# Dilated mixer: the values of two head groups projected as [dims, tokens] and turned by transposes, in place of products with strided stationary tokens

## The chip, the cores and the metric

The kernel runs on one core of one Trainium2 chip. The metric is the device time of one execution in microseconds, the median of several runs. Before the change it is 3231.49 us.

## The reference, cut to what matters

The network is an encoder of four layers for 512 tokens of width 1024 in float32. Each layer has a mixer and a SwiGLU block, each with a norm before and after it. The mixers are of kind A, B, C, A. The change touches kind A alone, which runs twice:

```python
def mixer_a(x, wqkv, wo):
    B, S, _ = x.shape
    qkv = (x @ wqkv).reshape(B, S, 3, A_NG, A_HEADS, A_HEAD_DIM)
    ...
    for g, (window, dilation) in enumerate(A_GROUPS):
        o, l = dilated_window_attention(qkv[:, :, 0, g], qkv[:, :, 1, g], qkv[:, :, 2, g], window, dilation, slopes[g])
    ...
    wgt = jax.nn.softmax(jnp.stack(lses, axis=0), axis=0)
    o = jnp.sum(wgt[..., None] * jnp.stack(outs, axis=0).astype(jnp.float32), axis=0)
    return o.reshape(B, S, -1).astype(x.dtype) @ wo
```

There are three groups (window and dilation 128 and 1, 512 and 4, 2048 and 16), each with 16 heads of 64 dims and with queries, keys and values of its own. In the second and third group a token sees only tokens at a distance that is a multiple of 4 or 16, so that one token in four forms a block of 128 that attends to itself.

## The kernel before, in words

Every product is made from float32 operands that are split into a high and a low part (`split`, L135: ScalarE copies the high part, VectorE subtracts it). `mm3` (L169) makes one product with three matmuls: high by high (L171), high by low (L172), low by high (L173). The normed input lies transposed in `yh` and `yl` as [dims, tokens], 8 slices of 128 dims (`KD`), 512 tokens and 64 more that repeat the first ones.

`wload` (L157) brings 1024 values a partition of weights from DRAM into a tile `raw` (3 buffers) by a DMA of SyncE, and splits it in two halves to `whi` and `wlo` (4 buffers each, L137 and L138).

Mixer A works by pairs of heads, p = 0 to 7. For each pair there are six projections of queries and keys (`proj_qk`, three groups, queries and keys): the weights stand still, 128 columns at a time, and the 512 tokens move. Each is 8 steps of three matmuls with 512 moving columns, into one PSUM bank of the tag "a" (the pool has 2 buffers for each tag). The values must come out with tokens as rows, so `vproj` lets the tokens stand still and moves the weights: 4 blocks of 128 tokens, 8 slices, three matmuls with 256 moving columns, 96 in all. `proj_v0` does this for the first group, once for four heads, with 128 tokens in order. `proj_v12` does it for groups two and three of one pair, and there a block is one token in four: `slice(c, S, 4)`. Its weights come as two tiles, each by two DMAs of 256 KB.

The order on TensorE is the emitted order. Attention goes in 64 units (pair, head, half of the blocks): `scores(n)`, `values(n - 2)`, `transposes(n - 1)`. Between these, `fill.run(part)` emits projection work from the generator `filler()` for as much estimated time as `part` says; a projection step of 0.65 us of estimate is yielded for each three matmuls with 512 columns or each six with 256. The order in `filler` is: queries and keys of group one (p+1), values of group one (every second pair), queries and keys of groups two and three (p+1), values of groups two and three (p+1). Buffers with one copy set gates: `wait(n)` stops the generator until unit n has been emitted. The second half of `proj_v12(p)` waits for unit 8p + 2, since `v12` of the pair before is read up to then; `proj_qk(p, 0, s)` waits for unit 8p - 5 before its bank is emptied. `fill.until` emits what a unit needs, without regard to the estimate. On ScalarE, VectorE and the queues a planner sets the order at build time.

`transposes` (L624) turns the softmax numerators by four transposes of 128 x 128 into one bank, and two splits move them to `pT`. `qk_evac` (L519) empties the banks of queries and keys; for groups two and three it reads the bank with a stride of four, `"p (l r) -> p r l"` (L534, L539).

Of the kernel before, what the change touches and what calls it, by code (L numbers as in the profile page):

```python
# [10 lines left out]
F32 = mybir.dt.float32  # L11
F32R = mybir.dt.float32r
AF = mybir.ActivationFunctionType
# [3 lines left out]
P = 128  # L17
S = 512
D = 1024
NB = S // P  # L20
KD = D // P
# [16 lines left out]
def const_tables():  # L38
    """Tables that depend on shapes alone."""
    f = np.float32  # L40
    q = np.arange(P)[:, None]
    w = np.arange(2 * P)[None, :]
    d0 = np.abs(w - 64 - q)
    t0 = np.where(d0 <= 64, d0, BIG).astype(f)
    l = np.arange(P)[None, :]
    d1 = np.abs(l - q)
    t1 = np.where(d1 <= 64, 4.0 * d1, BIG).astype(f)
    t2 = np.where((l - q) % 4 == 0, 4.0 * d1, BIG).astype(f)
    dist = np.concatenate([t0, t1, t2], axis=1)

    def angles(pos, dim):
        half = dim // 2
        fr = np.power(f(10000.0), -np.arange(half, dtype=f) * f(2.0) / f(dim)).astype(f)
        return (pos.astype(f)[:, None] * fr[None, :]).astype(f)

    t = np.arange(S)
    cs, sn = [], []
    for pos in (t // 64, t % 64):
        a = angles(pos, 64)
        c, s = np.cos(a), np.sin(a)  # L60
        cs += [c, c]
        sn += [-s, s]
    bcos = np.concatenate(cs, axis=1).astype(f)
    bsin = np.concatenate(sn, axis=1).astype(f)

    a = angles(t, 32)
    c, s = np.cos(a).astype(f), np.sin(a).astype(f)
    ccos = np.concatenate([c, c], axis=1)
    csin = np.concatenate([-s, s], axis=1)
    sc = f(96.0 ** -0.5)  # L70
    cq = np.empty((P, S), f)
    cq[:64] = -sc
    cq[64:96] = -(ccos.T * sc)
    cq[96:] = -(csin.T * sc)
    return {
        "t_dist": dist,
        "t_bcos": bcos,
        "t_bsin": bsin,
        "t_ckr": np.concatenate([ccos, csin], axis=1),
        "t_cq": cq,  # L80
    }


class Filler:
    """Work of the tensor engine that is emitted between the steps of something else."""
# [22 lines left out]
class Net:  # L108
# [32 lines left out]
    def behind(self, *ins):  # L141
        """What is emitted inside is issued after ins on their engines."""
        es = ExitStack()
        for i in ins:
            es.enter_context(self.tc.issue_after(i.ins))
        return es
# [10 lines left out]
    def wload(self, src, shape, pool=None, bufs=2):  # L157
        """Weights from DRAM as [128, ...] with at most 1024 values a partition, split."""
        n = int(np.prod(shape))
        raw, hi, lo = self.wtiles(pool, bufs)  # L160
        names = "abc"[: len(shape)]
        view = lambda x: x[:, :n].rearrange(
            f"p ({' '.join(names)}) -> p {' '.join(names)}", **dict(zip(names, shape)))
        self.nc.sync.dma_start(out=view(raw), in_=src)
        for c in (slice(0, n // 2), slice(n // 2, n)):
            self.split(hi[:, c], lo[:, c], raw[:, c])
        return view(hi), view(lo)
# [13 lines left out]
    def rstd(self, ss, n, count):  # L181
        """(ss / count + eps) ^ -0.5 for a [128, n] tile of sums."""
        nc = self.nc
        v = self.small.tile([P, 8], F32, tag="var", name=self.uid("var"))
        nc.vector.tensor_scalar(v[:, :n], ss, 1.0 / count, EPS, op0=ALU.mult, op1=ALU.add)
        r = self.small.tile([P, 8], F32, tag="rstd", name=self.uid("rstd"))
        nc.gpsimd.tensor_tensor(r[:, :n], v[:, :n], self.mhalf[:, :n], op=ALU.pow)
        return r
# [31 lines left out]
    def norm_t(self, t, yn, wrap):  # L220
        """Transposes of one block of tokens into yh, yl."""
# [13 lines left out]
    def rest(self, n=1):  # L235
        """Emits the loads of the next n blocks of the input."""
        for _ in range(min(n, len(self.loads))):
            self.loads.pop(0)()

    def flush(self, n=NB):  # L240
        """Emits the next n of the transposes that the stage before has left."""
        for _ in range(min(n, len(self.pending))):
            self.pending.pop(0)()

# [1 line left out]
    def rows_out(self, yp, stat, nf, w, acc_in, final, late=None, R=5):  # L246
        """y = stat^T @ w for [nf * 128, 1024] w. stat(f) gives the two parts [128, 512].
        final is None: the sums go to acc_in. Else (post gain, next pre gain or None, wrap).
        late: called before the products of the last f of the first half. A generator of PE time in us."""
        nc = self.nc  # L250
# [51 lines left out]
        # first half  # L302
# [26 lines left out]
        # second half  # L329
# [93 lines left out]
    def mixer_a(self, j, final):  # L423
        """Pairs of heads. The first group's blocks of queries are 128 tokens in order ("nat"), the other
        two groups share blocks of one token in four ("perm"). Both parts come out as [dims, tokens]."""
# [20 lines left out]
        def vproj(wt, dst, tok):  # L446
            for cp in range(2):
                bk = self.bank("a")
                for ci in range(2):
                    tb = tok(2 * cp + ci)  # L450
# [8 lines left out]
        def proj_v0(u):  # L459
            """Values of heads 4u..4u+3, first group: rows are keys."""  # L460
# [10 lines left out]
            g = vproj(wt, dst, lambda c: slice(64 + c * P, 192 + c * P))  # L471
            yield from gated(g, 8, 16 * u - 2)
            done.add(("v0", u))

        def proj_v12(p):
            """Values of a pair of heads, the other groups."""
            c0 = 2 * 3072 + 1024
            wt = []
            for kk in range(2):
                raw, hi, lo = self.wtiles()  # L480
                rv = raw.rearrange("p (k g c) -> p k g c", k=4, g=2)
                for g in range(2):
                    cg = c0 + g * 1024 + p * P
                    nc.sync.dma_start(out=rv[:, :, g, :], in_=w[kk * 512:(kk + 1) * 512, cg:cg + P]
                                      .rearrange("(k p) c -> p k c", p=P))
                for c in (slice(0, 512), slice(512, 1024)):
                    self.split(hi[:, c], lo[:, c], raw[:, c])
                wt.append([x.rearrange("p (k f) -> p k f", k=4) for x in (hi, lo)])

            def dst(cp, bk):  # L490
                if cp == 0:
                    st["v12"] = [new(f"v12{i}", [P, NB, 256]) for i in range(2)]
                t = [x[:, 2 * cp:2 * cp + 2, :] for x in st["v12"]]
                self.split(t[0], t[1], bk.rearrange("p (c e) -> p c e", c=2))

            g = vproj(wt, dst, lambda c: slice(c, S, 4))
            yield from gated(g, 8, 8 * p + 2)
            done.add(("v12", p))

        def gated(gen, n, unit):  # L500
            """The n-th item of gen is passed on before unit, the ones after it wait."""
# [50 lines left out]

        def filler():
            yield from proj_v0(0)
            yield from proj_v12(0)
            for p in range(1, 8):
                for s in range(2):
                    yield from proj_qk(p, 0, s, 8 * p - 5)
# [7 lines left out]
                yield from proj_v12(p)  # L566

# [100 lines left out]
        def weigh(p):  # L668
            """What each part counts for, from their maxima and sums."""
# [19 lines left out]
        def spread(p):  # L689
            """The weights as rows of tokens, on all partitions of their head."""  # L690
# [12 lines left out]
        def spread_fast(p):  # L703
            """The same by way of the tensor engine alone."""
# [38 lines left out]
        # first pair: columns of the first two blocks of tokens ahead  # L743
# [82 lines left out]
    def dense(self, ap, heads, get, M, G, before, each, end, lt=3, lv=5):  # L826
        """Steps of heads x blocks of queries: scores, then transposes, then products with the values,
        each some steps behind. G blocks of queries go into one product with the values. With M of 64 the
        first of v has the two parts of the values side by side, and the second one has the high part."""
# [73 lines left out]
    def mixer_tail(self, eo, es, w, final, ready, before_last=None, src=None):  # L903
        """The out projection as work to emit between the last steps of the heads."""
# [19 lines left out]
    def mixer_b(self, j, final):  # L924
# [33 lines left out]
        def rope(bk, n, t, who, dst, d0):  # L958
            """n heads of block t from a bank; transposed into dst[.][:, d0:d0+n, t]."""
# [91 lines left out]
        # a head's result takes the place of its queries  # L1051
# [217 lines left out]
    def run(self, stages):  # L1269
        """stages: list of (kind, mixer index, layer)."""  # L1270
# [12 lines left out]
        with self.tc.tile_pool(name="gp", bufs=1, reuse_waits="tile") as gp:  # L1283
# [19 lines left out]
            def warm(n):  # L1303
                """Keeps the tensor engine busy until there is something for it, for the sake of its clock."""
# [20 lines left out]
MANUAL = "AF"  # stages whose order on the tensor engine is the emitted one  # L1325
# [33 lines left out]
```

## Time and profile before

| | |
|---|---|
| median of 3 runs | 3231.49 us (3231.39 to 3234.03) |
| span of the profiled execution | 3234.7 us |
| TensorE busy | 3196.8 us, 99% |
| VectorE busy | 1546.5 us, 48% |
| ScalarE busy | 1401.5 us, 43% |
| GpSimd busy | 418.0 us, 13% |
| HBM read | 264.04 MB, 82 GB/s over the span |

The profile is of one execution. A timeline row gives the start and the duration in us, the engine, the line and the operation, then out<-in with the moving operand first and the stationary one second, the partitions and the shape. PE is TensorE's matmul, PEld its weight load. Matmuls overlap in the pipeline, so what one costs in a stream is the distance from its start to the start of the next, not its duration. A group's row has the count, then the busy time and the mean duration in ns, then the idle time of the engine before them.

### The profile page before, as it was taken

To read this page: it belongs to the slowest core of one execution; us is meant where nothing else is said; L and a number is where in the kernel's file an instruction comes from. 1 tells how busy PE (TensorE), PEld (TensorE's weight loads), DVE (VectorE), ACT (ScalarE), POOL (GpSimd) and SP (SyncE) were. 2 spreads that over 40 slices of the span, in tenths; PEclk is the share of its full clock that TensorE was granted. 3 is DMA by queue.
4 is the path that set the end of the run, shared out by engine and by line. 5 is a ranking of instruction groups with operands and counts; after the bars stand their busy time and mean duration, and the time that the engine had idled before them with its cause. 6 is when DMAs were issued, how large, how long until landed. Compare 5 with 4: busy or idle time off the path is not lost.

```text
span 3234.7 us, 43535 instructions
## 1 busy us (share of the span) xinstructions
PE 3196.8 (99%) x16742; PEld 2770.2 (86%) x16742; DVE 1546.5 (48%) x3120; ACT 1401.5 (43%) x3041; POOL 418.0 (13%) x628
## 2 busy tenths in 40 slices
PE   9999999999999999999999999999999999999998
PEld 8898998888887888888888888888999999888886
DVE  4445445543235864323578633345444455553233
ACT  4445444443234554223477632335444454543232
POOL 1011111020002221000254300003011010120000
PEclk9999999999999999999999999999999999999999
DMA  4222222233233213323211233232122222233332
GB/s 134 59 74 78 73 66 76 83 95 101 92 98 93 79 47 105 98 91 101 81 49 40 84 106 98 91 111 75 53 72 73 73 79 71 75 98 92 98 98 72
DMA packets 287328, 269.21 MB, mean 83 GB/s; under 512 B 10288, under 2 KB 247056, under 8 KB 287120
## 3 DMA queue, kind: packets, MB, share of 16 engines
q1 hardware_dynamic: 281248, 250.84, 25.4%
q0 software_dynamic: 5872, 15.59, 1.8%
q8 instruction: 132, 2.16, 0.3%
q14 instruction: 76, 0.62, 0.1%
HBM read 264.04 MB, written 2.34 MB: 82 GB/s over the span
## 4 chain that ended last, share of the span: by engine, by line
PE 61%; DVE 2%; issue 1%; ACT 1%; POOL 1%; DMA 0%; DVEq 0%; POOLq 0%; ACTq 0%
PE psa L173 9%; PE psa L172 9%; PE psa L171 9%; PE pss L171 4%; PE pss L172 4%; PE pss L173 4%; PE pso L172 3%; PE pso L173 3%; PE pso L171 3%; PE psp L173 3%; PE psp L171 3%; PE psp L172 3%; PE psp L853 1%; PE psp L624 1%; DVE wlo L138 1%
## 5 line engine op out<-in xcount | busy, mean ns | idle before, releaser
L138 DVE TENSOR_TENSOR wlo<-raw,whi 128x512 fp32r<-128x512 f32 (+1 forms) x895 | 590.6, 699 | 780.9 <-ACT whi L137 758.0
L137 ACT ACTIVATE whi<-raw 128x512 fp32r<-128x512 f32 (+2 forms) x928 | 524.1, 613 | 663.2 <-PE pss L172 140.8
L171 PE MATMUL psa<-yh,whi 128*128 128x512 f32 (+1 forms) x1152 | 447.6, 389 | 0.2 <-ACT yh L137 0.2
L172 PE MATMUL psa<-yl,whi 128*128 128x512 f32 (+1 forms) x1152 | 437.1, 379 | 6.8 <-DVE yl L138 6.8
L173 PE MATMUL psa<-yh,wlo 128*128 128x512 f32 (+1 forms) x1152 | 437.4, 380 | 0.0
L171 PE MATMUL psa<-whi,yh 128*128 128x256 f32 (+3 forms) x924 | 338.9, 367 | 2.8 <-ACT junk L964 2.0
L173 PE MATMUL psa<-whi,yl 128*128 128x256 f32 (+3 forms) x924 | 335.2, 363 | 3.5 <-DVE yl L138 3.5
L172 PE MATMUL psa<-wlo,yh 128*128 128x256 f32 (+3 forms) x924 | 335.6, 363 | 0.0
L173 PEld LDWEIGHTS psa<-whi,yl 128*128 128x128 f32 x924 | 247.7, 268 | 10.7 <-DVE yl L138 5.3
L171 PEld LDWEIGHTS psa<-whi,yh 128*128 128x128 f32 x924 | 246.4, 267 | 9.3 <-ACT junk L964 2.2
L173 PEld LDWEIGHTS psa<-yh,wlo 128*128 128x128 f32 x1152 | 216.7, 188 | 42.6
L172 PEld LDWEIGHTS psa<-yl,whi 128*128 128x128 f32 x1152 | 217.4, 189 | 40.9 <-DVE yl L138 9.0
L172 PEld LDWEIGHTS psa<-wlo,yh 128*128 128x128 f32 x924 | 247.6, 268 | 4.9
L171 PEld LDWEIGHTS psa<-yh,whi 128*128 128x128 f32 x1152 | 217.2, 189 | 32.4 <-ACT yh L137 0.5
L217 POOL TENSOR_TENSOR r<-v,mhalf 128x1 f32<-128x1 f32 x64 | 38.6, 604 | 1494.3 <-DVE v L215 1493.2
L138 DVE TENSOR_TENSOR pT<-psp,pT 128x512 fp32r<-128x512 f32 x128 | 88.1, 688 | 165.5 <-ACT pT L137 165.0
L171 PE MATMUL pss<-yh,whi 128*128 128x512 f32 (+1 forms) x448 | 160.9, 359 | 0.0
L173 PE MATMUL pss<-yh,wlo 128*128 128x512 f32 (+1 forms) x448 | 160.7, 359 | 0.0
L172 PE MATMUL pss<-yl,whi 128*128 128x512 f32 (+1 forms) x448 | 160.7, 359 | 0.0
L171 PE MATMUL pso<-yh,whi 128*128 128x512 f32 (+1 forms) x384 | 143.2, 373 | 0.0
L173 PE MATMUL pso<-yh,wlo 128*128 128x512 f32 (+1 forms) x384 | 142.6, 371 | 0.0
L171 PE MATMUL psp<-yh,whi 128*128 128x512 f32 (+1 forms) x384 | 142.6, 371 | 0.0
(418 smaller groups left out, 6665.2 us busy)
## 6 DMA issues: line engine op xcount, KB each, us to landing
raw<-a_wqkv SPq DMA_DIRECT2D x112, 512.0 KB, 3.6
raw<-ffn_wg SPq DMA_DIRECT2D x88, 512.0 KB, 3.5
raw<-ffn_wu SPq DMA_DIRECT2D x88, 512.0 KB, 3.5
raw<-ffn_wd SPq DMA_DIRECT2D x88, 512.0 KB, 3.8
raw<-a_wqkv SPq DMA_DIRECT2D x64, 256.0 KB, 3.3
raw<-a_wo SPq DMA_DIRECT2D x16, 512.0 KB, 3.9
wb<-scw POOLq DMA_DIRECT2D x28, 256.0 KB, 3.9
raw<-b_wqkv SPq DMA_DIRECT2D x12, 512.0 KB, 3.7
```

Source lines behind the costliest of these rows:

```text
L137: x = nc.scalar.activation(hi, src, AF.Copy)
L138: y = (eng or nc.vector).tensor_tensor(lo, src, hi.bitcast(F32), op=ALU.subtract)
L171: nc.tensor.matmul(out, sh, mh, start=start, stop=False)
L172: nc.tensor.matmul(out, sh, ml, start=False, stop=False)
L173: nc.tensor.matmul(out, sl, mh, start=False, stop=stop)
L217: nc.gpsimd.tensor_tensor(r, v, self.mhalf[:, 0:1], op=ALU.pow)
L624: nc.tensor.transpose(tp[:, (2 * i + c) * P:(2 * i + c + 1) * P], pp[:, i, c * P:(c + 1) * P], self.ident)
L853: nc.tensor.transpose(tp[:, c * P:(c + 1) * P], x[:, c * P:(c + 1) * P], self.ident)
```

## The change

`vproj` keeps only the first group's use. `proj_v12` now takes groups two and three one after the other, each with the helpers of queries and keys: 128 columns of weights stand still, 512 tokens in order move, and the bank holds [dims, tokens]. ScalarE copies the bank to a tile `vt` in SBUF (a buffer of the tag "yn", which has 2), and puts the tokens of one block side by side as it does so. Four transposes turn `vt` into another bank of the tag "a", and a split writes `v12`. The transposes of the second group come after the third step of the third group's projection; those of the third group are left in `st["turn"]` and come after the second step of the next projection (`after`), or at the end of `filler`. The gate at unit 8p + 2 now stands between the two groups. The remaining hunks drop comments and docstrings.

```diff
-        def vproj(wt, dst, tok):
+        def vproj(wt, dst):
...
-                    tb = tok(2 * cp + ci)
+                    tb = slice(64 + (2 * cp + ci) * P, 192 + (2 * cp + ci) * P)
...
         def proj_v12(p):
-            c0 = 2 * 3072 + 1024
-            wt = []
-            for kk in range(2):
-                raw, hi, lo = self.wtiles()
-                rv = raw.rearrange("p (k g c) -> p k g c", k=4, g=2)
-                for g in range(2):
-                    cg = c0 + g * 1024 + p * P
-                    nc.sync.dma_start(out=rv[:, :, g, :], in_=w[kk * 512:(kk + 1) * 512, cg:cg + P]
-                                      .rearrange("(k p) c -> p k c", p=P))
-                for c in (slice(0, 512), slice(512, 1024)):
-                    self.split(hi[:, c], lo[:, c], raw[:, c])
-                wt.append([x.rearrange("p (k f) -> p k f", k=4) for x in (hi, lo)])
-
-            def dst(cp, bk):
-                if cp == 0:
+            vt = {}
+
+            def turn(g):
+                bk = self.bank("a")
+                for c in range(NB):
+                    nc.tensor.transpose(bk[:, c * P:(c + 1) * P], vt[g][:, c * P:(c + 1) * P], self.ident)
+                if g == 1:
                     st["v12"] = [new(f"v12{i}", [P, NB, 256]) for i in range(2)]
-                t = [x[:, 2 * cp:2 * cp + 2, :] for x in st["v12"]]
-                self.split(t[0], t[1], bk.rearrange("p (c e) -> p c e", c=2))
-
-            g = vproj(wt, dst, lambda c: slice(c, S, 4))
-            yield from gated(g, 8, 8 * p + 2)
-            done.add(("v12", p))
+                t = [x[:, :, (g - 1) * P:g * P] for x in st["v12"]]
+                self.split(t[0], t[1], bk.rearrange("p (c e) -> p c e", c=NB))
+
+            for g in (1, 2):
+                wt = qk_load(g, 2, p)
+                bk = self.bank("a")
+                for k in range(KD):
+                    qk_mm(bk, wt, slice(0, S), k)
+                    yield 0.65
+                    if g == 2 and k == 2:
+                        turn(1)
+                        yield 0.45
+                vt[g] = self.work.tile([P, D], F32, tag="yn", name=self.uid("vt"))[:, :S]
+                nc.scalar.activation(vt[g].rearrange("p (r l) -> p r l", r=NB),
+                                     bk.rearrange("p (l r) -> p r l", r=NB), AF.Copy)
+                if g == 1:
+                    yield from wait(8 * p + 2)
+
+            def rest():
+                turn(2)
+                done.add(("v12", p))
+
+            st["turn"] = rest
...
+        def after(gen):
+            for i, c in enumerate(gen):
+                yield c
+                if i == 1 and "turn" in st:
+                    st.pop("turn")()
+                    yield 0.45
+
         def filler():
             yield from proj_v0(0)
             yield from proj_v12(0)
             for p in range(1, 8):
-                for s in range(2):
-                    yield from proj_qk(p, 0, s, 8 * p - 5)
+                yield from after(proj_qk(p, 0, 0, 8 * p - 5))
+                yield from proj_qk(p, 0, 1, 8 * p - 5)
                 done.add(("x", p))
...
                 yield from proj_v12(p)
+            st.pop("turn")()
```

More of the change, by code (lines that the diff above doesn't have):

```diff
@@ L469, in dst @@
                 self.split(t[:, :, :, 0, :], t[:, :, :, 1, :], bk.rearrange("p (c h e) -> p c h e", c=2, h=4))
-            g = vproj(wt, dst, lambda c: slice(64 + c * P, 192 + c * P))
-            yield from gated(g, 8, 16 * u - 2)
+            yield from gated(vproj(wt, dst), 8, 16 * u - 2)
             done.add(("v0", u))
         def proj_v12(p):
-            c0 = 2 * 3072 + 1024
-            wt = []
-            for kk in range(2):
-                raw, hi, lo = self.wtiles()
-                rv = raw.rearrange("p (k g c) -> p k g c", k=4, g=2)
-                for g in range(2):
-                    cg = c0 + g * 1024 + p * P
-                    nc.sync.dma_start(out=rv[:, :, g, :], in_=w[kk * 512:(kk + 1) * 512, cg:cg + P]
-                                      .rearrange("(k p) c -> p k c", p=P))
-                for c in (slice(0, 512), slice(512, 1024)):
-                    self.split(hi[:, c], lo[:, c], raw[:, c])
-                wt.append([x.rearrange("p (k f) -> p k f", k=4) for x in (hi, lo)])
```

## The prediction

> **What bounds the kernel now.** I read the page first: the busy line, the granted clock, the chain that ended last, the costliest groups.
>
> ```profile
> span 3234.7 us, 43535 instructions
> PE 3196.8 (99%) x16742; PEld 2770.2 (86%) x16742; DVE 1546.5 (48%) x3120; ACT 1401.5 (43%) x3041; POOL 418.0 (13%) x628
> PEclk9999999999999999999999999999999999999999
> PE 61%; DVE 2%; issue 1%; ACT 1%; POOL 1%; DMA 0%; DVEq 0%; POOLq 0%; ACTq 0%
> L137 ACT ACTIVATE whi<-raw 128x512 fp32r<-128x512 f32 (+2 forms) x928 | 524.1, 613 | 663.2 <-PE pss L172 140.8
> L138 DVE TENSOR_TENSOR wlo<-raw,whi 128x512 fp32r<-128x512 f32 (+1 forms) x895 | 590.6, 699 | 780.9 <-ACT whi L137 758.0
> L171 PE MATMUL psa<-whi,yh 128*128 128x256 f32 (+3 forms) x924 | 338.9, 367 | 2.8 <-ACT junk L964 2.0
> L171 PEld LDWEIGHTS psa<-whi,yh 128*128 128x128 f32 x924 | 246.4, 267 | 9.3 <-ACT junk L964 2.2
> L171 PEld LDWEIGHTS psa<-yh,whi 128*128 128x128 f32 x1152 | 217.2, 189 | 32.4 <-ACT yh L137 0.5
> ```
>
> TensorE is busy 99% of the span, at a granted clock of nine tenths or more in each slice, and the chain stays on it. Only less TensorE time, or new idle time on it, can move the end. One group is odd: the weight loads of `psa<-whi,yh`, where tokens stand still, take 267 ns on average, the same loads of `psa<-yh,whi` 189 ns. A mean can mix two kinds, so I went to the timeline where the first group's values (`proj_v0`) give way to those of the other two (`proj_v12`).
>
> ```profile
> 60.16 0.28 PE L172 MATMUL psa<-wlo,yh 128*128 128x256 f32 x1
> 60.16 0.19 PEld L173 LDWEIGHTS psa<-whi,yl 128*128 128x128 f32 x1
> ...
> 63.16 0.28 PE L173 MATMUL psa<-whi,yl 128*128 128x256 f32 x1
> ...
> 67.13 0.40 PE L172 MATMUL psa<-wlo,yh 128*128 128x256 f32 x1
> 67.23 0.33 PEld L173 LDWEIGHTS psa<-whi,yl 128*128 128x128 f32 x1
> ...
> 75.07 0.40 PE L173 MATMUL psa<-whi,yl 128*128 128x256 f32 x1
> ```
>
> From 60.16 to 63.16 lie 25 matmuls of the first group: 3.00 / 25 = 0.120 us from start to start. From 67.13 to 75.07 lie 34 of the same shape with tokens four apart: 7.94 / 34 = 0.2335 us, and each load takes 0.33 us instead of 0.19. The two streams differ in the tokens' stride alone, and nothing waits in either: the dear loads set the pace.
>
> **The change part by part.**
>
> *Removed.* Two mixers x 8 pairs x 4 blocks x 8 slices x 3 = 1536 matmuls at 0.2335 us: 358.7 us.
>
> *Added products.* Two mixers x 8 pairs x 2 groups x 8 x 3 = 768 matmuls with 512 moving columns, weights standing still. That is the form of the queries and keys:
>
> ```profile
> 273.73 0.42 PE L171 MATMUL psa<-yh,whi 128*128 128x512 f32 x1
> ...
> 274.44 0.39 PE L171 MATMUL psa<-yh,whi 128*128 128x512 f32 x1
> ...
> 276.49 0.22 PE L171 MATMUL pso<-pT,v 128*64 128x128 f32 x1
> ```
>
> Twelve of them fill the 2.76 us from the first row to the last: 0.230 us each, and 768 cost 176.6 us. The last nine alone, from 274.44, take 2.05 us, 0.228 each; that is the low end.
>
> *Added transposes.* 32 sets of four, in the form of L624:
>
> ```profile
> 84.61 0.60 PE L624 MATMUL psp<-ident,p 128*128 128x128 f32 x4
> 84.96 0.48 PE L171 MATMUL psa<-whi,yh 128*128 128x256 f32 x1
> 85.29 0.40 PE L172 MATMUL psa<-wlo,yh 128*128 128x256 f32 x1
> ```
>
> A set takes 0.35 us, and the matmul after it 0.33 us instead of 0.23: 0.45 us, and 32 sets 14.4 us. Not below 32 x 0.35 = 11.2 us, since nothing else runs on TensorE in that time.
>
> *Sum on TensorE.* 358.7 - 176.6 - 14.4 = 167.7 us saved, 10.5 us a pair.
>
> The Trainium skill's page "TensorE: Matmul & The Clock Gate", section "LDWEIGHTS (loading the stationary operand)", speaks against this: it times a load by its columns alone, P / 1.2, which for 128 columns is 107 ns whatever their stride. By it the old matmuls would run at the pace of the first group and the change would lose a few microseconds (the last rival, below). The measured 0.33 beside 0.19 us decides for the stride.
>
> *Added copies.* 32 copies of a bank to `vt` on ScalarE, read with a stride of four. The eviction of the queries of groups two and three reads a bank the same way; the split of `v12` reads one in order:
>
> ```profile
> L539 ACT ACTIVATE y<-psa x60: 572/592/596, 47.4 to 2770.8; 64x512 fp32r<-64x512 f32 x60
> 64.33 1.14 ACT L137 ACTIVATE whi<-raw 128x512 fp32r<-128x512 f32 x2
> 75.51 0.60 ACT L137 ACTIVATE v<-psa 128x512 fp32r<-128x512 f32 x1 [6.93 <-PE psa L173]
> ```
>
> 0.59 us strided, 0.60 in order: I take 0.59, and 32 x 0.59 = 18.9 us of ScalarE. Splits stay as they are: two weight tiles and two banks a pair, 512 wide, before and after. The same skill's page "SBUF — State Buffer", section "Door 1: The DMA port swizzle (why `[64,N]` ≈ `[32,N]`)", says that PSUM lines hold two float32 values and that non-contiguous access to PSUM slows matmuls much; the copy is no matmul, and the two rows here show no price for it.
>
> What hides the copy is the time until its transposes. The last product started at 75.07, ScalarE began its read of the bank at 75.51 and ended at 76.11: 1.04 us. The first transposes come three steps later (10 x 0.23 = 2.30 us after that start), the second two steps later (7 x 0.23 = 1.61 us), so both are covered when ScalarE is free, by 1.26 and 0.57 us. With one weight tile's split ahead of the copy (1.14 us) the second would be 0.57 us late, the first not. I take 0.2 us for each of the 32 turns, an estimate between 0 and, with one such split and one more 0.60 us ahead, 1.2 us: 6.4 us, bounds 0 and 38 us. Behind a waiting transpose stands all of TensorE, and so the next unit's scores.
>
> *Weights.* These are the engines' loads by stretch and over both mixers:
>
> ```profile
> 0.00:674.00 674.00, 663.28 (x3825) 603.14 (x3826) 339.31 (x773) 326.95 (x746) 90.61 (x177) 1.00 0.27 79
> 2205.00:2862.00 657.00, 651.13 (x3761) 592.35 (x3761) 331.09 (x758) 318.62 (x723) 91.99 (x173) 1.00 0.26 74
> 239.10:263.30 24.20, 24.20 (x151) 20.80 (x150) 15.13 (x35) 15.55 (x37) 5.77 (x11) 1.00 0.36 107
> 283.70:307.00 23.30, 23.30 (x106) 23.30 (x105) 7.62 (x24) 6.37 (x17) 0.59 (x2) 1.00 0.08 23
> raw<-a_wqkv SPq DMA_DIRECT2D x112, 512.0 KB, 3.6
> raw<-a_wqkv SPq DMA_DIRECT2D x64, 256.0 KB, 3.3
> L171 PE MATMUL psa<-yh,whi 128*128 128x512 f32 x352 | 143.3, 407 | 0.0
> ```
>
> (Window rows: time; busy PE, PEld, DVE, ACT, POOL; clock, DMA share, GB/s. The last row is of the first mixer's products, 0 to 660 us.) A tile was used for 48 x 0.2335 = 11.2 us and will be used for 24 x 0.23 = 5.5 us. The stretch from 239.10 has that pace already: ScalarE 64% busy, 107 GB/s, TensorE busy throughout, and in the whole mixer the products of queries and keys waited 0.0 us. The stretch of the old values, from 283.70, has 27% and 23 GB/s. So there is room: cost 0. On SyncE's queue the 64 DMAs of 256 KB become 32 of 512 KB; none is moved past another kind. The second group's tile is asked for behind the gate instead of with the first, which matters only if the planner doesn't run ahead (a rival). Over both mixers ScalarE goes from 645.6 of 1331 us (49%) to about 664 of 1169 (57%), VectorE from 670.4 (50%) to 57%: neither becomes the bound. The clock was 1.00 in both kinds of stretch, so a denser stream isn't charged.
>
> *Total.* 167.7 - 6.4 = 161.3, say 162 us. From the profiled span, 3234.7, that leaves 3072.7; the median of the runs is 3.2 us lower, and the difference is as good there: 3231.5 - 162 = **3069.5 us**.
>
> **The rivals.**
>
> *The banks of "a" become the bound* (0.16). A turn takes one of two banks in the midst of a projection. If banks go strictly in turn, the second group's projection and the next one (and that one and its successor) fall into the same bank, and TensorE waits for it to be emptied. Such an eviction of queries has two ScalarE reads of 0.59 us: 0.44 + 2 x 0.59 + 0.70 (VectorE's part, at the split's price) = 2.3 us, and one copy to `vt` 0.8 us after its product's slot. Seven pairs a mixer have both: 14 x 3.1 = 43 us, time 3231.5 - 161 + 43 = 3113. If a bank is taken as it comes free, nothing of this happens. The trace has no odd number of banks in a row from which to tell. Late copies at their bound of 38 us give 3102; the case spans 3090 to 3125.
>
> *Weights arrive late* (0.04), the case on the other side. If both tiles of a pair are split only when TensorE stands at them, each costs 3.6 + 2 x 0.613 + 0.70 = 5.5 us, and with two late turns (2 x 1.2) that is 13.4 us a pair against 10.5 saved: 16 x 2.9 = 46 us slower, 3278. It turns into a loss beyond 10.5 us a pair. With the second tile alone late, 16 x 5.5 = 88 us are lost and 3157 is left. Against it: 0.0 us of waiting in products that are fed the same way.
>
> *The stride isn't what makes the loads dear* (0.02), so that the change does not do what it says. Then the old matmuls cost 1536 x 0.120 = 184.3 against 191.0 us, and the time is 3238, 7 us up, hardly to be told from no change. Only the two streams quoted speak to it, and they speak against.
>
> **How the numbers follow.** The forecast's own case gets 0.78: from 3056 (no late turn, 0.228 us a product, transposes at 11.2 us: 358.7 - 175.1 - 11.2 = 172.4 saved, 3059, and 3 us for what differs from one execution to another, as the span and the median do) to 3090 (two thirds of the bound on turns). Bank waits reach on to 3125, and the range takes the lower half of them: 3056 to 3105. Outside lie about 0.08 of the banks, 0.06 of the other two and 0.04 of the tails. A measurement here can tell some 0.2%, 6.5 us, from no change. Faster 0.94 (own case and banks), same 0.02 (no effect of the stride), slower 0.04 (late weights, whole).
>
> **What would show it.** Right: in the changed profile the 0.33 us loads of `psa<-whi,yh` are gone and only the 0.19 us kind is left, 768 more products of 512 columns stand at 0.23 us, 128 transposes of `vt` in sets of 0.35 us, TensorE is still 98 to 99% busy, and each mixer is some 80 us shorter. Wrong by the first rival: idle time ahead of `psa<-yh,whi` released by ScalarE or VectorE, or ahead of the transposes of `vt`. Wrong by the second: idle time there released by `wlo`. Wrong by the third: the new products cost as much as the old. A granted clock below 0.99 in the mixers would be outside all of them.

## The result and the profile after

| | before | after |
|---|---|---|
| median | 3231.52 us (4 runs, 3231.39 to 3234.03) | 3086.10 us (4 runs, 3083.49 to 3088.32) |
| span of the profiled execution | 3234.7 us | 3084.3 us |

The ratio is 0.9548, 95% interval 0.9534 to 0.9561: faster by 145.4 us in the medians, 150.4 us in the profiled spans. The forecast was 3069.5 us with a range from 3056 to 3105. The time lies in the range, 16.6 us above the forecast.

The page of the kernel after: the span, the busy line, the granted clock, the chain that ended last by engine, and the group of the products with moving tokens.

```profile
span 3084.3 us, 42241 instructions
PE 3035.5 (98%) x16102; PEld 2570.6 (83%) x16102; DVE 1551.5 (50%) x3120; ACT 1418.4 (46%) x3073; POOL 422.5 (14%) x628
PEclk9999999999999999999999999999999999999999
PE 61%; DVE 2%; ACT 1%; issue 1%; POOL 1%; POOLq 0%; DVEq 0%; ACTq 0%
L171 PE MATMUL psa<-yh,whi 128*128 128x512 f32 (+1 forms) x1408 | 552.2, 392 | 0.2 <-ACT yh L137 0.2
```

The group has 256 instructions more than before, which for its three lines makes the 768 new products. TensorE is busy 161.3 us less, and 98% in place of 99%.

The instructions on the tile `yh` in the kernel after (minimum, median and maximum of one in ns):

```profile
L171 PEld LDWEIGHTS psa<-whi,yh x412: 186/189/192, 51.5 to 2680.0; 128*128 128x128 f32 x138
```

No load of stationary tokens of this line takes longer than 192 ns any more. A turn in the timeline of TensorE:

```profile
72.61 0.60 PE L482 MATMUL psa<-ident,vt 128*128 128x128 f32 x4
72.97 0.47 PE L171 MATMUL psa<-yh,whi 128*128 128x512 f32 x1
73.28 0.39 PE L172 MATMUL psa<-yl,whi 128*128 128x512 f32 x1
73.51 0.40 PE L173 MATMUL psa<-yh,wlo 128*128 128x512 f32 x1
```

0.36 us for the four, 0.31 us for the matmul after them: what the prediction took from L624. So the parts of the sum are there. What was not foreseen stands in the waits of TensorE, here those of the first mixer before (20 to 660 us) and after (20 to 590 us): who waited for whom, us in total, times, the longest.

```profile
PE psa L173 <- DVE yl L138: 2.2, 2, 2.1
PE pso L172 <- DVE pT L138: 0.7, 1, 0.7
```

```profile
PE pss L610 <- ACT kh L538: 2.4, 2, 1.4
PE pss L611 <- POOL kl L540: 2.2, 2, 1.1
PE psa L482 <- ACT vt L498: 1.9, 3, 1.5
PE pso L172 <- DVE pT L138: 1.7, 1, 1.7
PE psa L173 <- DVE yl L138: 0.2, 1, 0.2
```

The turns waited 1.9 us for `vt`. But the scores (`pss`, L610 and L611, the old L592 and L593) now waited 4.6 us for the keys, which they never did before, and one product with the values waited 1.0 us longer. The second mixer has the same rows: 2.4, 2.2, 1.9 and 1.6 us.

After these waits the clock falls. Windows of 3.41 us of the kernel after, around two of the waits, and two more at half the clock (the columns: time; busy PE, PEld, DVE, ACT, POOL; granted clock; DMA share; GB/s):

```profile
346.81:350.22 3.41, 1.67 (x17) 1.27 (x16) 3.32 (x9) 1.58 (x5) 0.00 (x0) 1.00 0.54 159
350.23:353.64 3.41, 3.41 (x14) 2.82 (x13) 1.52 (x3) 0.60 (x1) 0.15 (x1) 0.50 0.00 0
357.05:360.46 3.41, 1.41 (x8) 0.76 (x6) 2.61 (x4) 3.23 (x7) 1.50 (x3) 1.00 0.18 32
360.47:363.88 3.41, 3.34 (x9) 2.79 (x10) 1.40 (x5) 1.54 (x5) 0.62 (x2) 0.50 0.44 130
493.59:497.00 3.41, 3.41 (x19) 3.01 (x19) 1.40 (x5) 1.48 (x5) 0.61 (x1) 0.50 0.32 120
2606.44:2609.85 3.41, 3.41 (x20) 2.92 (x19) 1.40 (x5) 1.16 (x5) 0.61 (x1) 0.50 0.25 88
```

In this kernel each stretch in which TensorE was busy for less than half is followed by one at half the clock (the last section shows where this does not hold). There are four half-clock stretches in the two mixers, each worth up to 1.7 us.

### The profile page after: what moved, and what is told of

The parts are those of the page before. It is cut to its first block, busy times and chain, and to the rows that moved or that the text cites. A ratio compares the mean times of both kernels' runs of the same rounds, so it can differ in the third digit from the quotient of the medians.

```text
span 3084.3 us, 42241 instructions
## 1 busy us (share of the span) xinstructions
PE 3035.5 (98%) x16102; PEld 2570.6 (83%) x16102; DVE 1551.5 (50%) x3120; ACT 1418.4 (46%) x3073; POOL 422.5 (14%) x628
## 4 chain that ended last, share of the span: by engine, by line
PE 61%; DVE 2%; ACT 1%; issue 1%; POOL 1%; POOLq 0%; DVEq 0%; ACTq 0%
PE psa L171 8%; PE psa L172 8%; PE psa L173 8%; PE pss L171 4%; PE pss L172 4%; PE pss L173 4%; PE pso L172 3%; PE pso L171 3%; PE pso L173 3%; PE psp L171 3%; PE psp L173 3%; PE psp L172 3%; PE psp L871 1%; PE psp L642 1%; DVE wlo L138 1%
## 5 line engine op out<-in xcount | busy, mean ns | idle before, releaser
L171 PE MATMUL psa<-yh,whi 128*128 128x512 f32 (+1 forms) x1408 | 552.2, 392 | 0.2 <-ACT yh L137 0.2
L172 PE MATMUL psa<-yl,whi 128*128 128x512 f32 (+1 forms) x1408 | 538.2, 382 | 6.9 <-DVE yl L138 6.9
L173 PE MATMUL psa<-yh,wlo 128*128 128x512 f32 (+1 forms) x1408 | 538.8, 383 | 0.0
L172 PEld LDWEIGHTS psa<-yl,whi 128*128 128x128 f32 x1408 | 266.6, 189 | 48.9 <-DVE yl L138 9.0
L137 ACT ACTIVATE hT<-sg 128x512 fp32r<-128x512 f32 x88 | 55.0, 625 | 198.4 <-DVE sg L405 198.4
L172 PE MATMUL psp<-yl,whi 128*128 128x512 f32 (+1 forms) x384 | 142.6, 371 | 0.0
L173 PE MATMUL psp<-yh,wlo 128*128 128x512 f32 (+1 forms) x384 | 142.6, 371 | 0.0
L172 PE MATMUL pso<-yl,whi 128*128 128x512 f32 (+1 forms) x384 | 142.5, 371 | 0.0
L171 PE MATMUL psa<-whi,yh 128*128 128x256 f32 (+3 forms) x412 | 134.6, 327 | 2.3 <-ACT junk L982 1.5
L173 PE MATMUL psa<-whi,yl 128*128 128x256 f32 (+3 forms) x412 | 131.7, 320 | 0.3 <-DVE yl L138 0.3
```

What stands on the lines that cost most here:

```text
L137: x = nc.scalar.activation(hi, src, AF.Copy)
L171: nc.tensor.matmul(out, sh, mh, start=start, stop=False)
L172: nc.tensor.matmul(out, sh, ml, start=False, stop=False)
L173: nc.tensor.matmul(out, sl, mh, start=False, stop=stop)
```

## The experiments

**Theory.** The turns carry an estimate of 0.45 us each, 0.9 us a pair, while the shares that `run(part)` hands out stayed as they were. So the projections slide by 0.9 us of estimate a pair. After some pairs the keys of the next pair are emptied from their bank right ahead of the scores that need them, TensorE stands, and the clock is halved behind it. **Rival.** The slide has no effect; ScalarE and VectorE, with 57% of the mixers, are fuller and something waits anyway.

**The estimates put to 0.**

```diff
-                        yield 0.45
+                        yield 0.0
...
-                    yield 0.45
+                    yield 0.0
```

> The change with the two estimates of 0.45 us for a set of transposes put to 0, so that the projections are emitted at the units where they stood before the change; no instruction is added or removed. Theory (the shortfall against 168 us comes from projections that slid by 0.9 us of estimate a pair, until the queries and keys of a later pair are emptied right before the scores that need them, with idle time there and half-clock stretches behind it): idle time before the scores gone, no half-clock stretch inside a mixer, median near 3070 us, 3066 to 3076. Rival (ScalarE and VectorE are simply fuller now, and something waits wherever the projections stand): same as the change, 3086, within 5 us.

Measured: 3067.98 us (4 runs, 3067.54 to 3068.35), ratio 0.9489 (0.9475 to 0.9503). Instructions and data are those of the change; only the order on TensorE differs, and what the planner makes of it on the other engines. The waits of its first mixer, 20 to 580 us, and the stretch from 300 to 500 us, first here and then in the change:

```profile
PE psa L482 <- ACT vt L498: 2.6, 3, 2.0
PE pso L172 <- DVE pT L138: 0.7, 1, 0.7
PE psa L173 <- DVE yl L138: 0.2, 1, 0.2
```

```profile
300.00:500.00 200.00, 199.40 (x1179) 170.59 (x1178) 114.04 (x270) 114.17 (x264) 25.14 (x58) 1.00 0.28 82
```

```profile
300.00:500.00 200.00, 193.51 (x1123) 164.82 (x1123) 107.90 (x252) 108.03 (x246) 25.97 (x54) 0.97 0.28 79
```

The waits of the scores are gone, the clock is 1.00 in place of 0.97, and TensorE stands 0.6 us in these 200 us in place of 6.5. ScalarE and VectorE are fuller here than in the change (114 us against 108, since more of the program fits into the same 200 us), and yet TensorE hardly waits.

The slide can be seen at one place, the keys of the sixth pair: ScalarE's last reads of their bank (`kh`; first one head, then the other) and the pair's first scores, in the kernel before, in the change, and with estimates of 0.

```profile
407.81 0.59 ACT L529 ACTIVATE kh<-psa 64x512 fp32r<-64x512 f32 x1
412.41 0.25 PE L592 MATMUL pss<-kh,q 128*128 128x192 f32 x1
```

```profile
357.85 0.58 ACT L537 ACTIVATE kh<-psa 64x512 fp32r<-64x512 f32 x1
358.44 0.59 ACT L538 ACTIVATE kh<-psa 64x512 fp32r<-64x512 f32 x1
359.08 0.35 PE L610 MATMUL pss<-kh,q 128*128 128x192 f32 x1 [0.97 <-ACT kh L538]
...
360.38 0.59 ACT L538 ACTIVATE kh<-psa 64x512 fp32r<-64x512 f32 x1
360.54 0.53 PE L611 MATMUL pss<-kl,q 128*128 128x192 f32 x1 [1.10 <-POOL kl L540]
```

```profile
355.16 0.59 ACT L538 ACTIVATE kh<-psa 64x512 fp32r<-64x512 f32 x1
359.77 0.25 PE L610 MATMUL pss<-kh,q 128*128 128x192 f32 x1
```

Before, the last read, for the second head, ended 412.41 - 408.40 = 4.0 us ahead of the pair's first scores. In the change the reads for the first head end at 359.03, and the scores of that head wait for its keys piece by piece: for the high part until 359.08, for the low part until 360.54. The last read, for the second head, starts only at 360.38, behind the first scores. With estimates of 0 the lead is 359.77 - 355.75 = 4.0 us again.

**The estimates doubled**, to 0.9 us, by the same two lines.

> The opposite: the estimates put from 0.45 to 0.9 us, so that the projections slide twice as far. Theory of the slide: more scores wait for keys, and the time is above the change's by 5 to 30 us, 3091 to 3116. Rival of full engines: 3086, within 5 us.

Measured: 3099.22 us (4 runs, 3096.84 to 3103.22), ratio 0.9587 (0.9571 to 0.9603). Its waits in the first mixer:

```profile
PE pss L610 <- ACT kh L538: 4.6, 3, 1.6
PE pss L611 <- POOL kl L540: 3.3, 3, 1.1
```

7.9 us at three pairs in place of 4.6 us at two. With 0, 0.45 and 0.9 us of estimate the times are 3068, 3086 and 3099 us. The instructions are the same in all three, so the slide decides.

**More work for ScalarE**, on top of the estimates of 0: each bank is copied once more, to a tile that is not read.

```diff
+                nc.scalar.activation(self.work.tile([P, 512], F32, tag="junk", name=self.uid("junk"), bufs=1), bk, AF.Copy)
```

> The turns at an estimate of 0, as in the run before, and in addition every bank that is copied to vt is copied once more to a tile that nobody reads, after the first copy: 32 x 0.6 = 19 us more on ScalarE, all outputs as they were. Theory of the slide: the engines' load isn't what decides, 3068 us, up to 3 us more. Rival of full engines: idle time comes back on TensorE, 3075 us or more.

Measured: 3072.16 us (4 runs, 3070.89 to 3073.29), ratio 0.9504 (0.9489 to 0.9520). That is 4.2 us more, between the two expectations. (This run ran on another chip than the one with estimates of 0, as did those of the step of three and of the last two experiments; the kernel before took 3232.2 us there and 3232.7 us here.) The first mixer's waits tell what it was:

```profile
PE psa L482 <- ACT junk L500: 1.8, 3, 0.8
PE psa L482 <- ACT vt L498: 1.7, 1, 1.7
PE pso L172 <- DVE pT L138: 0.7, 1, 0.7
```

```profile
968.79:972.20 3.41, 3.41 (x9) 2.65 (x9) 3.21 (x12) 0.00 (x0) 0.85 (x1) 0.50 0.00 0
```

No scores wait. The turns wait 3.5 us in place of 2.6, some of it for the second copy, which holds the bank longer; in the second mixer it is 3.5 in place of 2.3 us. That is 2.1 us. The window row shows a half-clock stretch outside the mixers, which adds up to 1.7 us. It follows a wait of 2.0 us that the other kernels have there too (1.5 to 2.0 us). The kernel with estimates of 0 keeps the full clock behind it (first two rows), and the kernel before does not (third row):

```profile
964.38:967.79 3.41, 1.50 (x7) 1.29 (x8) 3.41 (x10) 1.40 (x6) 0.00 (x0) 1.00 0.00 0
967.80:971.21 3.41, 3.41 (x17) 2.83 (x16) 3.21 (x14) 0.00 (x0) 0.85 (x1) 1.00 0.00 0
```

```profile
1051.00:1054.41 3.41, 3.41 (x9) 2.65 (x10) 3.38 (x11) 0.23 (x2) 0.36 (x1) 0.50 0.02 5
```

So this stretch can't be put down to the second copy. 19 us of further ScalarE work thus cost some 2 us of waiting, of 4.2 us measured, and not by the waits that the change had.

**Is it the stride?** Three runs of the kernel before, with other tokens standing still: 128 in order, two apart, three apart.

```diff
-            g = vproj(wt, dst, lambda c: slice(c, S, 4))
+            g = vproj(wt, dst, lambda c: slice(c * P, (c + 1) * P))
```

```diff
+            g = vproj(wt, dst, lambda c: slice(c % 2 + 256 * (c // 2), 256 + 256 * (c // 2), 2))
```

```diff
+            g = vproj(wt, dst, lambda c: slice(c, c + 3 * P - 2, 3))
```

> The kernel before, with the stationary tokens of groups two and three taken 128 in order instead of one in four; this gives the values of groups two and three for other tokens than the reference has, and changes no instruction's shape or count. If the stride makes the loads dear: 1536 matmuls at 0.120 instead of 0.2335 us, 174 us less, 3057 us, loads of 0.19 us. If it is not the stride: 3231 us, loads of 0.33 us.

> The kernel before, with stationary tokens two apart instead of four (again values of other tokens than the reference's in groups two and three). If a load pays for each 16 bytes that it touches beyond two float32 values a line, as the Trainium skill's page SBUF - State Buffer, section Door 1, has it, a stride of two costs nothing: 0.120 us a matmul, 3057 us. If the price grows with the stride: half of the surplus, 0.18 us, near 3144 us.

> The kernel before, with stationary tokens three apart (values of other tokens than the reference's in groups two and three). A line of 16 bytes then holds one token or two, on average 1.33. If each new line costs about a fixed time: between the pace of stride two (3060 us) and that of stride four (3232 us); pays per line in proportion: 3/4 lines a token against 1/2 and 1, near 3146 us. If only a load with less than two tokens in every line is dear, it comes out as dear as stride four, near 3232 us.

Measured, one run each: 3058.90, 3060.36 and 3144.48 us. In order, the first mixer's loads of stationary tokens (0 to 600 us) are all of the cheap kind; two apart, the median over the whole run is 194 ns:

```profile
L171 PEld LDWEIGHTS psa<-whi,yh 128*128 128x128 f32 x396 | 75.6, 191 | 1.3 <-ACT yh L137 0.8
```

```profile
L171 PEld LDWEIGHTS psa<-whi,yh x924: 186/194/330, 51.6 to 2654.4; 128*128 128x128 f32 x185
```

Three apart, a stretch of products:

```profile
66.33 0.34 PE L172 MATMUL psa<-wlo,yh 128*128 128x256 f32 x1
...
69.31 0.34 PE L171 MATMUL psa<-whi,yh 128*128 128x256 f32 x1
```

17 matmuls in 2.98 us, 0.175 us each. With steps of 4, 8, 12 and 16 bytes a matmul thus costs 0.120, about 0.120, 0.175 and 0.2335 us. The stride alone accounts for 3232.7 - 3058.9 = 173.8 us (3232.7 is the kernel before beside that run), and 1536 x 0.1135 = 174.3 us was the expectation. The Trainium skill's page "SBUF — State Buffer", section "Door 1: The DMA port swizzle (why `[64,N]` ≈ `[32,N]`)", has lines of 16 bytes, of which two hits are needed for full bandwidth. The runs agree: two tokens a line cost nothing that is seen, one token a line twice as much. They do not agree with the free stride of 4 float32 values that the same passage gives, since that is the step that costs twice as much here. Counted by lines, 128 tokens touch 128 lines at a step of 16 bytes and 96 at a step of 12: 0.2335 / 128 = 1.82 ns a line, and 96 x 1.82 = 0.175 us, as measured. A price that rises evenly from a step of 8 bytes to one of 16 would give 0.177 us at 12; the runs don't tell the two apart, and no larger step was run.

**What the turning costs.** Estimates of 0, and `v12` split straight from the projection's bank, without copies and transposes:

```diff
-                bk = self.bank("a")
-                for c in range(NB):
-                    nc.tensor.transpose(bk[:, c * P:(c + 1) * P], vt[g][:, c * P:(c + 1) * P], self.ident)
+                bk = vt[g]
...
-                vt[g] = self.work.tile([P, D], F32, tag="yn", name=self.uid("vt"))[:, :S]
-                nc.scalar.activation(vt[g].rearrange("p (r l) -> p r l", r=NB),
-                                     bk.rearrange("p (l r) -> p r l", r=NB), AF.Copy)
+                vt[g] = bk
```

> The turns at an estimate of 0, and with the copies to vt and all transposes of them left out: v12 is split straight from the projection's bank and so holds values that are not turned, which changes the result of groups two and three. Measures what the turning costs as it stands: by the prediction 32 sets at 0.45 us, 14.4 us, and by the traces 4.9 us of waiting for copies, together 19 us: 3049 us. If transposes cost more than their place on TensorE (through banks or ScalarE): below 3045 us.

Measured, one run: 3051.21 us. That is 16.8 us less than with turns: the transposes at their place on TensorE and a few us of waiting, nothing beyond.

**The last turn later**, with estimates of 0:

```diff
             cur.run(part)
+            if n == 60:
+                st.pop("turn")()
...
-            st.pop("turn")()
...
-                bk = self.bank("a")
+                bk = self.bank("p" if (p, g) == (7, 2) else "a")
```

> The turns at an estimate of 0, and the last pair's second turn of each mixer is put behind the first products of the out projection (its transposes go to a bank of the tag p), in place of right behind its copy, where the transposes waited 2.0 and 1.7 us. Expected: that wait gone or under 0.5 us, 3 to 4 us less than 3068, so 3064 to 3065 us.

Measured: 3066.61 us (4 runs, 3066.27 to 3067.41), ratio 0.9488 (0.9474 to 0.9503). 1.4 us less than 3067.98, where 3 to 4 had been expected, and the two intervals of the ratio are nearly the same. The wait for `vt` went from 2.6 to 0.6 us in the first mixer, but another of 0.8 us, for `yl`, came behind it near the mixer's end. By its median it is the fastest of the kernels that leave nothing out, though hardly to be told from the one with estimates of 0.

```profile
PE psa L173 <- DVE yl L138: 1.0, 2, 0.8
PE psa L482 <- ACT vt L498: 0.6, 2, 0.3
```

Not run: a second `yh` with the tokens sorted, so that the old products would read them in order. It needs 32 KB a partition beside the mixer's tiles; whether there is room for it was not tried.

## Why the prediction was right, and where it was off

**The mechanism held.** The strided loads set the pace of the old products: run in order, the same instructions save 173.8 us. The third rival, that the stride doesn't matter, is refuted by that run.

**The sum on TensorE held.** It gave 167.7 us, and with estimates of 0 the kernel is 3232.7 - 3068.0 = 164.7 us faster (medians on the same chip), though its turns still wait 2.6 + 2.3 = 4.9 us. The set of transposes at 0.45 us and the product at 0.230 us stand.

**The step that failed is the price of waiting.** The prediction put 6.4 us on it, all at the turns, and none on "Weights", where it found room on the engines and concluded "cost 0". In the traces of both mixers the turns waited 1.9 + 1.9 = 3.8 us, less than the allowance. The scores waited 2 x 4.6 = 9.2 us, one product with the values a mixer 1.0 and 0.9 us longer, and four half-clock stretches lost up to 4 x 1.7 = 6.8 us. That is up to 21.7 in place of 6.4 us. The run with estimates of 0 puts the price of the slide at 3086.1 - 3068.0 = 18.1 us. On the other side a wait of 2.1 us near the end of the first mixer, with a half-clock stretch behind it, is no longer there, up to 3.7 us gained:

```profile
621.00:624.30 3.30, 3.30 (x21) 3.20 (x20) 2.05 (x7) 0.65 (x2) 0.00 (x0) 0.50 0.00 0
```

(That row is the kernel before, right behind its wait.) The half-clock stretch of the kernel before at 1051.00 is gone as well, up to 1.7 us more.

The net can be read from the two pages. TensorE's idle time, the span less its busy time, rose from 37.9 to 48.8 us, by 10.9 us. The half-clock stretches went from two to four, up to 3.4 us. The busy time fell by 161.3 us, so without the clock's part by some 164.7 us, 3.0 us less than the sum. 164.7 - 10.9 - 3.4 = 150.4 us, the difference of the spans. Waiting and clock took 14.3 us net, 7.9 us more than the prediction had for them. The rest of the 16.6 us has other sources: the 3.0 us of the sum, 0.7 us from calling 161.3 us 162, and 5.0 us from the step from span to median. The prediction took 3.2 us between the two for both kernels, but in the change the span lies 1.8 us below the median: the execution that was profiled before took longer than its kernel's median, the one after did not.

The cause of the slide is an edit that stands in the diff and that the prediction did not cost: the two `yield 0.45`. They aren't work, but they are charged against the shares that decide behind which unit a projection is emitted. 0.9 us a pair was enough: in the stretch from 300 us the keys came right at their scores. The room on the engines, which was real, didn't help, since the order on TensorE is fixed when the kernel is built.

**Luck.** That the time lay in the range is in part luck. The upper end of the prediction's own case, 3090, was kept for late turns; these took 3.8 us, and the slide, which had no price at all, happened to fit into the same room.

**The first rival did not happen.** The banks would show as products `psa<-yh,whi` waiting for ScalarE or VectorE in the middle of a mixer. The first mixer's waits have no such row beyond those of the kernel before. Its band, 3090 to 3125, held the run with doubled estimates, by another cause. **The second** did not either: no product waited for `wlo`.

**The clock.** The prediction argued that a denser stream would not lower the clock, and called a clock below 0.99 outside all its cases. With estimates of 0 the clock is 1.00 from 300 to 500 us, as argued. In the change it was 0.97 there: the half-clock stretches stand right behind the waits, as the windows above show, and not in the dense stretches.

## What to carry to other kernels

Where a timeline shows weight loads of one shape with two durations, look at the step between the stationary columns: here 16 bytes cost twice as much as 8. When work is added to a filler with budgets, its estimate moves everything behind it; follow the next deadline of what is moved, and charge nothing (raising the budgets to match was not run). Where TensorE stands for some 1.7 us or more within one stretch of 3.41 us, the clock behind it can cost up to another 1.7 us.

## What the runs showed of the hardware

- The half-clock stretches lie on a grid of 3.4133 us: in the kernel after they begin at 350.23, 360.47, 493.59 and 2606.44 us, and the distances are 3, 39 and 619 times that. In the windows of the grid ahead of them TensorE was busy 1.67, 1.41, 0.92 and 0.91 us. Two windows with waits split between them stayed at full clock, at 2.43 and 2.31 us:

```profile
2469.90:2473.31 3.41, 2.43 (x18) 1.77 (x16) 1.46 (x3) 2.87 (x6) 1.54 (x3) 1.00 0.01 2
2473.32:2476.73 3.41, 2.31 (x12) 1.84 (x13) 2.54 (x7) 2.11 (x6) 1.21 (x2) 1.00 0.58 156
```

  The same pair of waits, 0.97 and 1.10 us, halved the clock when both fell into one window (357.05 to 360.46) and did not when the border lay between them. The Trainium skill's page "TensorE: Matmul & The Clock Gate", section "HAM oscillation — how this bites in real kernels", asks for no idle gap over some 3.4 us. Here a single gap of 1.7 us was enough, so the measured rows decide. The busy time of a window does not settle it alone, though: with estimates of 0 the clock stayed full behind a window with 1.50 us (the row from 964.38 above), less than the 1.67 us that were followed by half the clock. Where the border lies stays open.
- A bank read with a step of 16 bytes cost ScalarE nothing: the copies to `vt` took 0.59 us on 128 partitions, as an eviction in order does (0.60 us, the row of `v` in the prediction).

```profile
L498 ACT ACTIVATE vt<-psa x32: 575/590/607, 70.7 to 2647.6; 128x512 f32<-128x512 f32 x32
```
